# The attention stage of a hybrid decoder layer with its order written by hand, its scores negated, and other rules for the conditioning rows beside it

## The chip, the cores and the metric

The kernel runs on one NeuronCore of a Trainium2 chip. The metric is device time in microseconds (us). The kernel before takes 1560.94 us, the median of three runs (1560.8 to 1561.51). In what follows PE is the matrix engine (TensorE), PEld its weight loads, DVE the vector engine, ACT the scalar engine, SP the engine that issues nearly all loads from device memory.

## What is computed

One decoder layer on 256 tokens of width 2048, float32 throughout:

```
mod = silu(c) @ w_ada + b_ada            # 6 x 2048 numbers: shift, scale, gate, twice
h = adaLN(RMSNorm(x))
lru_x, lru_gate, q, k, v, g_a, g_b = split(h @ w_in)
rec = rg_lru(conv4(lru_x))               # two gate products a 128-channel block, then a scan over tokens
y_a = (rec * gelu(lru_gate)) @ w_lru_out
# attention: 32 query heads, 4 key heads of 64, blocks of 128 tokens, window 128
logits = q k^T * 64^-0.5 + bias          # or -1e30 outside the window
m = max(max(logits), sink);  e = exp(logits - m)
p = e / (sum(e) + exp(sink - m));  att = p v
y_b = att @ w_attn_out
x = x + gate1 * ((sigmoid(g_a) * y_a + sigmoid(g_b) * y_b) @ w_out)
x = x + gate2 * (relu(adaLN(RMSNorm(x)) @ w_ff1)^2 @ w_ff2);  out = RMSNorm(x)
```

## The kernel before

Every large product is split in three: weights and activations are each rounded to the fp32r type with a remainder, and high by high, high by low and low by high are summed in PSUM. A weight tile of 128 by 2048 numbers (1 MB) is loaded by SP into one of four `raw` buffers, rounded by ACT in two halves of 1024 columns (`wh`, line 177) and its remainder is taken by DVE in two halves (`wl`, line 182). There are four `wh` and four `wl` halves, enough for two tiles.

The work is a list of *units*, one weight tile each. Units 0 and 1 make k and v, units 2 to 9 eight pairs of q tiles, units 10 to 17 eight pairs of the recurrence's input (lx), units 18 to 25 its gate branch (lg), units 26 to 53 the two branch gates, 54 to 69 the product with w_lru_out (`ya`), then `yb`, `out`, and the MLP. Up to unit 29 a unit is 48 matmuls of 256 columns (`gemm`, lines 203 to 205): two halves of 24, one for each output tile, each reading one 1024-column half of the weights. From unit 30 on a unit is 16 matmuls of 512 columns and 16 of 256 (`gemm_wide`, lines 228 to 231). The split of `q` or `lx` between a first part, made in a stage ahead of the units, and the rest means that a unit ends with an addition to `both[f]`.

Beside the units stand two other kinds of work. **Side work** (`later`) is queued with a cost and taken from the queue after each unit as long as a credit of 2.3 a unit lasts, capped at 6: attention for one group of four heads at a time (`att_scores`, cost 2.5, and `att_values`, cost 0.3; eight groups), then for each of 16 recurrence tiles a convolution (line 738), two gate products (lines 746 and 747), a decay and a scan, and a gelu. **Rows** (`ada_dma`, `ada_unit`) make the 96 columns of `mod`: one load of 1 MB into a `raw` buffer and one DVE instruction of 2048 columns (line 282). A second credit sets how many rows are issued with a unit: 0.2 a unit up to unit 7, then 0.5, none in the two units ahead of `ya`, and what is left spread evenly after that. The first `ya` unit also splits the 16 results of the recurrence (line 166), and `flush()` ahead of it takes all side work that is left.

Each engine runs its instructions in the order of its own queue. The program is written in the order above, and a scheduler then sets each engine's order, except that instructions under `pin` keep the order in which they are written. In the units of the kernel before almost nothing is pinned.

Attention for one group of four heads (`att_scores`): 16 small matmuls on PE (line 666) give scores in four PSUM banks; eight DVE instructions (line 671) add the bias and take each row's running maximum; DVE negates the eight maxima (675) and subtracts them from the sink (676); ACT takes the exponential of that (677) and the eight exponentials with their sums (681); DVE adds, inverts (683, 684) and scales (688, eight instructions). In `att_values` PE transposes the four heads (703, twelve), ACT copies them to SBUF (705), PE multiplies with v (710, sixteen) and ACT copies the result (712).

## Time and profile before

| what | value |
|---|---|
| runs, median (lowest to highest) | 1560.94 us (1560.8 to 1561.51) |
| the profiled execution's own time | 1560.38 us |
| its span in the trace | 1558.6 us |
| PE busy | 1540.5 us, 99% of the span |
| DVE busy | 1287.1 us, 83% |
| ACT busy | 926.2 us, 59% |
| granted TensorE clock, mean | 0.998 |
| bytes moved | 387.93 MB, 249 GB/s on average |

Times in the trace are us from the span's start. A row of a group has the line of the kernel, the engine, the operation, what it writes and reads, its count, then busy time and the mean duration of one in ns, then the idle time of its engine ahead of it. A row of the list of waits says who waited for whom, how many us in total, how many times, and the longest. A row of the timeline has start, duration, engine, line and count, and in brackets how long the engine was idle ahead of it and what ended that. A row of windows has a stretch, its length, and for each engine the busy time and in brackets the number of instructions, then the granted clock, the share of the DMA engines and GB/s. Matmuls overlap: each lasts longer than the distance to the next one's start.

### The profile page before, as it was taken

What the parts mean: (1) busy time and instruction counts of PE and PEld (TensorE: products, weight loads), DVE (VectorE), ACT (ScalarE), POOL (GpSimd) and SP (SyncE); (2) the same over time, 40 slices, a digit from 0 to 9 for tenths busy, and PEclk for the clock granted to TensorE, in tenths of its full rate; (3) what the DMA queues carried; (4) which work ended last, traced back from release to release, by engine and by line L of the source; (5) the groups of instructions that cost most, each with busy time, mean ns of one, the idle gap of its engine ahead of it and who ended that gap; (6) DMA issues with size and microseconds to landing.
All of it is one profiled execution on the core that took longest, in us unless ns stands there. A gap on an engine that the chain in (4) does not pass through costs nothing.

```text
span 1558.6 us, 25695 instructions
## 1 busy us (share of the span) xinstructions
PE 1540.5 (99%) x10137; PEld 1396.9 (90%) x10137; DVE 1287.1 (83%) x2037; ACT 926.2 (59%) x1531; POOL 0.2 (0%) x4
## 2 busy tenths in 40 slices
PE   8999999999999999999999999999999999999998
PEld 7999999889988888888889988888988888888887
DVE  5898987889999888898898877888866887668885
ACT  5763456579886564444465763366744765357764
POOL 0000000000000000000000000000000000000000
PEclk9999999999999999999999999999999999999999
DMA  9999976545768777777876676865654556546551
GB/s 374 349 387 335 358 272 233 216 167 215 283 250 303 279 266 299 293 293 275 324 285 237 230 268 240 320 226 188 217 193 175 178 198 222 187 159 203 191 215 55
DMA packets 84744, 387.93 MB, mean 249 GB/s; under 512 B 7344, under 2 KB 36368, under 8 KB 44432
## 3 DMA queue, kind: packets, MB, share of 16 engines
q1 hardware_dynamic: 79632, 381.51, 67.3%
q10 hardware_dynamic: 4992, 4.79, 1.0%
q8 instruction: 79, 1.29, 0.3%
q14 instruction: 41, 0.34, 0.1%
HBM read 384.13 MB, written 2.15 MB: 248 GB/s over the span
## 4 chain that ended last, share of the span: by engine, by line
PE 92%; DVE 3%; DMA 2%; ACT 2%; issue 1%; SPq 0%; DVEq 0%; ACTq 0%
PE pg L229 41%; PE pg L228 20%; PE pg L205 5%; PE pg L203 5%; PE pg L204 5%; DMA ra<-in_wada_dram 1%; PE pg L231 1%; PE pa L938 1%; PE pa L940 1%; PE pa L939 1%; PE pg L985 1%; PE pg L986 1%; PE pg L987 1%; PE pa L710 1%; PE pa L703 1%
## 5 line engine op out<-in xcount | busy, mean ns | idle before, releaser
L229 PE MATMUL pg<-k,wh 128*128 128x512 f32 x2832 | 980.9, 394 | 1.1 <-DVE k L166 1.1
L177 ACT ACTIVATE wh<-rw 128x1024 fp32r<-128x1024 f32 (+1 forms) x542 | 560.2, 1041 | 481.1 <-PE pg L229 320.9
L182 DVE TENSOR_TENSOR wl<-rw,wh 128x1024 fp32r<-128x1024 f32 (+1 forms) x542 | 644.6, 1201 | 162.3 <-ACT wh L177 157.3
L228 PE MATMUL pg<-k,wl 128*128 128x256 f32 x2655 | 743.0, 280 | 0.0
L229 PEld LDWEIGHTS pg<-k,wh 128*128 128x128 f32 x2832 | 521.6, 188 | 107.4 <-issue 1.4
L228 PEld LDWEIGHTS pg<-k,wl 128*128 128x128 f32 x2655 | 499.0, 188 | 8.8 <-ACT k L165 0.7
L203 PE MATMUL pg<-k,wh 128*128 128x256 f32 x878 | 248.3, 283 | 0.0
L204 PE MATMUL pg<-k,wh 128*128 128x256 f32 x878 | 247.0, 282 | 0.0
L205 PE MATMUL pg<-k,wl 128*128 128x256 f32 x878 | 247.0, 282 | 0.0
L282 DVE CUSTOM_DVE_ANT_0 ra<-ra,scr,vc 128x2048 f32<-128x2048 f32 x96 | 225.3, 2347 | 12.0 <-DMA ra<-in_wada_dram 10.4
L203 PEld LDWEIGHTS pg<-k,wh 128*128 128x128 f32 x878 | 165.4, 188 | 1.9 <-issue 1.6
L205 PEld LDWEIGHTS pg<-k,wl 128*128 128x128 f32 x878 | 164.8, 188 | 1.7 <-issue 1.5
L204 PEld LDWEIGHTS pg<-k,wh 128*128 128x128 f32 x878 | 165.1, 188 | 0.6 <-issue 0.3
L1104 DVE SCALAR_TENSOR_TENSOR k<-pg,mod,k 128x256 f32<-128x256 f32 x100 | 48.3, 483 | 17.9 <-PE pg L229 16.4
L236 DVE TENSOR_TENSOR t<-pg,t 128x256 f32<-128x256 f32 x127 | 53.1, 418 | 0.5 <-ACT t L235 0.5
L231 PE MATMUL pg<-k,wl 128*128 128x256 f32 x177 | 49.6, 280 | 0.0
L235 ACT ACTIVATE t<-pg 128x256 f32<-128x256 f32 x127 | 46.3, 365 | 0.6 <-PE pg L229 0.6
L987 PE MATMUL pg<-z,wl 128*128 128x258 f32 x144 | 40.9, 284 | 0.0
L985 PE MATMUL pg<-z,wh 128*128 128x258 f32 x144 | 40.8, 284 | 0.0
L986 PE MATMUL pg<-z,wh 128*128 128x256 f32 x144 | 40.7, 283 | 0.0
L231 PEld LDWEIGHTS pg<-k,wl 128*128 128x128 f32 x177 | 33.4, 189 | 7.1
L166 DVE TENSOR_TENSOR k<-t,k 128x256 fp32r<-128x256 f32 x80 | 33.8, 422 | 1.9 <-ACT k L165 1.9
(216 smaller groups left out, 1351.6 us busy)
## 6 DMA issues: line engine op xcount, KB each, us to landing
rw<-in_w_f_dram SPq DMA_DIRECT2D x188, 1024.0 KB, 4.9
ra<-in_wada_dram SPq DMA_DIRECT2D x96, 1024.0 KB, 6.7
rw<-in_w_r_dram SPq DMA_DIRECT2D x30, 1024.0 KB, 5.0
rw<-in_w_p_dram SPq DMA_DIRECT2D x29, 960.0 KB, 6.9
rw<-in_w_f_dram SPq DMA_DIRECT2D x48, 256.0 KB, 3.3
bt<-ud ACTq DMA_DIRECT2D x8, 512.0 KB, 4.1
k<-in_w_p_dram SPq DMA_DIRECT2D x9, 256.0 KB, 10.8
lw<-in_lruw_dram SPq DMA_DIRECT2D x4, 512.0 KB, 5.7
```

The costliest lines, as they stand in the source:

```text
L177: pin(se.activation(wh[:, :c], raw[:, o:o + c], AF.Copy))
L182: pin(ve.tensor_tensor(out=wl[:, :c], in0=raw[:, o:o + c], in1=wh[:, :c].bitcast(F32), op=ALU.subtract))
L203: te.matmul(ps, lhsT=wh[:, w], rhs=hl[:, 0], start=k == 0, stop=False)
L204: te.matmul(ps, lhsT=wh[:, w], rhs=hl[:, 1], start=False, stop=False)
L205: te.matmul(ps, lhsT=wl[:, w], rhs=hl[:, 0], start=False, stop=k == n - 1)
L228: te.matmul(ps[:, 0], lhsT=wl[:, w], rhs=hl[:, 0], start=False, stop=False)
L229: te.matmul(ps, lhsT=wh[:, w], rhs=hl, start=k == 0, stop=k == n - 1)
L231: te.matmul(ps[:, 0], lhsT=wl[:, w], rhs=hl[:, 0], start=False, stop=False)
L282: pin(ve.tensor_tensor_reduce(out=raw, in0=raw, in1=scr, scale=1.0, scalar=vc[:, V_BADA + c:V_BADA + c + 1], op0=ALU.mult, op1=ALU.add, ac ...
L985: te.matmul(ps, lhsT=wh[:, e], rhs=z[k][:, 0:258], start=k == 0, stop=False)
L986: te.matmul(ps[:, 0:256], lhsT=wh[:, e], rhs=z[k][:, 258:514], start=False, stop=False)
L987: te.matmul(ps, lhsT=wl[:, e], rhs=z[k][:, 0:258], start=False, stop=k == KT - 1)
```

## The change

- **Attention in sixteen units.** Units 3 to 18 no longer go through the loop. `attention(ready)` writes eight groups, two units a group, with everything pinned: half of unit *a*, the scores, the second half of *a*, half of unit *b*, the transposes, the second half of *b*, the values. The rounding of the next group's weights, their remainders, their loads and one row stand at written places between. Before, eight groups were spread by credit over the units from 2 on and the scheduler set their place.
- **Scores negated.** q is scaled by -0.125, the bias line and the sinks are negated once, the DVE instruction takes a running minimum, and the result is the exponential's bias as it stands. The negation of eight maxima (line 675) is gone, and each exponential is written right behind its own DVE instruction; the exponential of the sink comes after the eight.
- **All transposes of a group together, all values together**, instead of two heads at a time.
- **Side work waits.** No side work is taken before unit 19; the credit stands at its cap of 6 by then. Attention is no longer in the queue.
- **Rows.** One a group in the attention units (eight), then 0.1 a unit up to unit 28 and 0.5 from unit 29 on; at most one a unit; none in the four units ahead of `ya` and its first three. By the loop's own arithmetic rows 1, 7, 16 and 28 fell in units 0 to 2, 3 to 18, 19 to 53 and 54 to 97; now it is 1, 8, 11 and 32, of which 13 fall one a unit in units 57 to 69.

The main parts of the diff:

```diff
-LAG, CC, CG, CV, CS = 2, 1.0, 0.6, 0.3, 2.5
+LAG, CC, CG = 2, 1.0, 0.6
+ATT, GROUPS, ATT_ROWS = 3, 8, [1] * 8
-LOOK, CREDIT, Z_FROM, ADA_RATE, ADA_SLOW, QUIET_ATT = 2, 2.3, 12, 0.5, 0.2, 8
+LOOK, CREDIT, Z_FROM, QUIET_YA = 2, 2.3, 12, 4
+ADA_RATES = 29 * [0.1] + 27 * [0.5]
...
-                    ve.tensor_tensor_reduce(out=s[:, sl], in0=pss[i][:, sl], in1=bt[:, 2 * t + i, 0:128 * (b + 1)],
-                                            scale=1.0, scalar=sink[:, c:c + 1], op0=ALU.add, op1=ALU.max,
-                                            accum_out=m[:, c:c + 1])
+                    pin(ve.tensor_tensor_reduce(out=s[:, sl], in0=pss[i][:, sl], in1=bt[:, 2 * t + i, 0:128 * (b + 1)],
+                                                scale=1.0, scalar=sink[:, c:c + 1], op0=ALU.add, op1=ALU.min,
+                                                accum_out=ng[:, c:c + 1]))
+                    table("exp", pin(se.activation(s[:, sl], s[:, sl], AF.Exp, scale=-1.0, bias=ng[:, c:c + 1],
+                                                   accum_out=dn[:, c:c + 1])))
...
+    def attention(ready):
+        nxt = {n: Half(n) for n in range(ATT + 2, ATT + 2 * GROUPS + 2)}
...
+        for g in range(GROUPS):
+            a, b = ATT + 2 * g, ATT + 2 * g + 1
+            for _ in range(ATT_ROWS[g]):
+                ada_dma(pin)
...
+            half(a, 0)
+            att_scores(g)
+            att_sink(g)
+            if g + 1 < GROUPS:
+                att_bias(g + 1)
+            half(a, 1)
+            fin(a)
+            att_scale(g)
+            na, nb = first(g + 1), second(g + 1)
+            na.round()
+            na.round()
+            half(b, 0)
+            att_turns(g)
+            na.rest()
+            na.rest()
+            if first(g + 2):
+                first(g + 2).ask()
+            for _ in range(ATT_ROWS[g]):
+                ada_unit(pin)
+            nb.round()
+            half(b, 1)
+            fin(b)
+            att_values(g)
+            nb.round()
+            nb.rest()
+            nb.rest()
+            if second(g + 2):
+                second(g + 2).ask()
...
+        if n == ATT:
+            stage[0] = pin
+            attention(ready)
+            stage[0] = same
+        if ATT <= n < ATT + 2 * GROUPS:
+            continue
...
-        if not (n_ya - 2 <= n < n_ya or n_ff1 - QUIET_OUT <= n < n_ff1 or n_ff1 + 16 - QUIET_FF1 <= n < n_ff1 + 16):
-            while ada_credit > rows and ada_next[0] + rows < 6 * KT:
+        if not (n_ya - QUIET_YA <= n < n_ya + 3 or n_ff1 - QUIET_OUT <= n < n_ff1 or n_ff1 + 16 - QUIET_FF1 <= n < n_ff1 + 16):
+            while ada_credit > rows and rows < 1 and ada_next[0] + rows < 6 * KT:
...
-        while credit > 0 and side:
+        while credit > 0 and side and n >= ATT:
```

**How the orders differ at three places.** First DVE, in the seventh group, from the last score instruction to the first scaling. `as` holds a group's maxima, sums and inverses, `wl` is a weight remainder, `ra` a row, `k_607<-pg_3821` a unit's closing addition. Before:

```order
L671 ISA t_3368,as_3346<-pa_3360,bt_3344,vc 128x256
L671 ISA as_3346 128x1
L182 TENSOR_TENSOR wl_3815<-rw_3811,wh_3813 128x1024
L675 TENSOR_SCALAR as_3346<-as_3346 128x8
L676 TENSOR_TENSOR as_3346<-vc,as_3346 128x8
L282 ISA ra_4044,mod<-ra_4044,scr,vc 128x2048
L282 ISA mod 128x1
L773 TENSOR_TENSOR k_607<-pg_3821,k_607 128x512
L683 TENSOR_TENSOR as_3346<-as_3346 128x8
L684 RECIPROCAL as_3346<-as_3346 128x8
L688 TENSOR_SCALAR t_3353<-t_3353,as_3346 128x128
```

and now:

```order
L683 ISA t_3774,as_3746<-pa_3764,bt_3575,nsink 128x256
L683 ISA as_3746 128x1
L693 TENSOR_TENSOR as_3746<-as_3746,nsink 128x8
L852 TENSOR_TENSOR k_668<-pg_3721,k_668 128x512
L699 TENSOR_TENSOR as_3746<-as_3746 128x8
L700 RECIPROCAL as_3746<-as_3746 128x8
L704 TENSOR_SCALAR t_3753<-t_3753,as_3746 128x128
```

The weight remainder and the row have left the stretch between scores and scaling; they stand behind the eight scalings now.

Second PE, at the transposes (`idt`) and values (`vtok`) of the sixth group; `wh`/`wl` rows are a unit's matmuls. Before:

```order
L205 MATMUL pg_3821<-k_1669,wl_3664 128x256
L703 MATMUL pa_3309<-idt,t_3207 128x128
L203 MATMUL pg_3821<-k_1766,wh_3662 128x256
L204 MATMUL pg_3821<-k_1766,wh_3662 128x256
L703 MATMUL pa_3309<-idt,t_3207 128x128 x2
L703 MATMUL pa_3315<-idt,t_3210 128x128 x3
```

and now (the second group, alike in all eight):

```order
L206 MATMUL pg_2792<-k_2207,wl_2683 128x256
L712 MATMUL pa_2817<-idt,t_2723 128x128 x3
L712 MATMUL pa_2823<-idt,t_2728 128x128 x3
L712 MATMUL pa_2829<-idt,t_2739 128x128 x3
L712 MATMUL pa_2835<-idt,t_2744 128x128 x3
L204 MATMUL pg_2792<-k_1175,wh_2681 128x256
```

Twelve transposes stand in one block at the middle of unit *b*, and 24 of that unit's matmuls lie between them and the values.

Third DVE ahead of the first `ya` unit, where the splits of the recurrence's results (`k_6450<-k_531` and after) begin. Before:

```order
L282 ISA ra_6436,mod<-ra_6436,scr,vc 128x2048
L282 ISA mod 128x1
L182 TENSOR_TENSOR wl_6345<-rw_6341,wh_6343 128x1024
L182 TENSOR_TENSOR wl_6349<-rw_6341,wh_6347 128x1024
L236 TENSOR_TENSOR t_6384<-pg_6351,t_6384 128x256
L282 ISA ra_6438,mod<-ra_6438,scr,vc 128x2048
L282 ISA mod 128x1
L182 TENSOR_TENSOR wl_6393<-rw_6389,wh_6391 128x1024
L166 TENSOR_TENSOR k_6450<-k_531,k_6450 128x256
```

and now:

```order
L183 TENSOR_TENSOR wl_6325<-rw_6317,wh_6323 128x1024
L237 TENSOR_TENSOR t_6360<-pg_6327,t_6360 128x256
L872 SCALAR_TENSOR_TENSOR t_6365<-t_6365,k_940 128x256
L183 TENSOR_TENSOR wl_6375<-rw_6371,wh_6373 128x1024
L874 SCALAR_TENSOR_TENSOR t_6365<-t_6365,k_940 128x256
L167 TENSOR_TENSOR k_6428<-k_532,k_6428 128x256
L875 SCALAR_TENSOR_TENSOR k_723<-t_6365,k_723 128x256
```

The two rows are gone from there, and the last steps of the last gelu (872, 874, 875) stand where none stood before.

More of the change, by code (lines that the diff above doesn't have):

```diff
@@ L404, in hybrid_layer @@
     relt = cp.tile([32, NH], F32, name="relt")
+    nsink = cp.tile([P, 2 * NH], F32, name="nsink")
     ud = dp.tile([32, 384], F32, name="ud")
@@ L646, in hybrid_layer, with att_bias @@
     ast = {}
+    stage = [same]
+    keep = lambda i: stage[0](i)
+    def att_bias(g):
+        bt = sp.tile([P, 4, T], F32, tag="bias", name=nm("bt"), bufs=1)
+        pin(se.dma_start(out=bt, in_=bass.AP(tensor=ud.tensor, offset=ud.offset + 4 * g * 384,
+                                             ap=[[1, P], [384, 4], [1, T]])))
+        ast[g] = bt
     def att_scores(g):
         kv = g // 2
-        bt = sp.tile([P, 4, T], F32, tag="bias", name=nm("bt"), bufs=1)
-        se.dma_start(out=bt, in_=bass.AP(tensor=ud.tensor, offset=ud.offset + 4 * g * 384,
-                                         ap=[[1, P], [384, 4], [1, T]]))
-        st = sp.tile([P, 4, 8], F32, tag="ast", name=nm("as"), bufs=2)
-        m, ng, dn, es = st[:, 0], st[:, 1], st[:, 2], st[:, 3]
+        bt = ast[g]
+        st = sp.tile([P, 3, 8], F32, tag="ast", name=nm("as"), bufs=2)
+        ng, dn = st[:, 0], st[:, 1]
         ss = []
-        sink = vc[:, V_SINK + 8 * g:V_SINK + 8 * g + 8]
+        sink = nsink[:, 8 * g:8 * g + 8]
         for t in range(2):
@@ L680, in att_scores @@
                 c = 2 * i + b
-                table("exp", se.activation(ss[i][:, sl], ss[i][:, sl], AF.Exp, bias=ng[:, c:c + 1],
-                                           accum_out=dn[:, c:c + 1]))
-        ve.tensor_tensor(out=dn, in0=dn, in1=es, op=ALU.add)
-        ve.reciprocal(out=dn, in_=dn)
-        for i in range(4):
-            for b, sl in HALVES:
-                c = 2 * i + b
-                ve.tensor_scalar(out=ss[i][:, sl], in0=ss[i][:, sl], scalar1=dn[:, c:c + 1], scalar2=None, op0=ALU.mult)
@@ L689, in att_scores, with att_turns @@
-        ast[g] = ss
+                pin(ve.tensor_scalar(out=ss[i][:, sl], in0=ss[i][:, sl], scalar1=dn[:, c:c + 1], scalar2=None,
+                                     op0=ALU.mult))
+    def att_turns(g):
+        pvs = []
+        for s in ast[g][0]:
+            pt = bank([P, 384])
+            for n, j in enumerate((0, 2, 1)):
+                pin(te.transpose(pt[:, n * P:(n + 1) * P], s[:, j * P:(j + 1) * P], idt))
+            pv = tmp([P, 384])
+            pin(se.activation(pv, pt, AF.Copy))
+            pvs.append(pv)
+        ast[g] = pvs
@@ L708, in att_values @@
             for kb, cols, pc in ((1, slice(0, 256), slice(0, 256)), (0, slice(128, 256), slice(256, 384))):
                 for i in range(2):
-                    te.matmul(po[64 * i:64 * i + 64, cols], lhsT=vtok[:, kb, vs], rhs=pvs[i][:, pc],
-                              start=kb == 1, stop=kb == 0)
-            se.activation(res[F_Q + 2 * g + t], po, AF.Copy)
-    def q_fin(f, ps, part):
-        ve.scalar_tensor_tensor(out=part, in0=ps, scalar=0.125, in1=part, op0=ALU.mult, op1=ALU.add)
-        if f > 0:
-            later(CV, att_values, f // 2 - 1)
-        later(CS, att_scores, f // 2)
-        if f == 14:
-            later(CV, att_values, 7)
+                    pin(te.matmul(po[64 * i:64 * i + 64, cols], lhsT=vtok[:, kb, vs], rhs=pvs[2 * t + i][:, pc],
+                                  start=kb == 1, stop=kb == 0))
@@ new lines, in attention, with half, fin @@
+    def attention(ready):
+        nxt = {n: Half(n) for n in range(ATT + 2, ATT + 2 * GROUPS + 2)}
+        first, second = lambda g: nxt.get(ATT + 2 * g), lambda g: nxt.get(ATT + 2 * g + 1)
+        first(1).ask()
+        second(1).ask()
+        att_bias(0)
+        for g in range(GROUPS):
+            a, b = ATT + 2 * g, ATT + 2 * g + 1
+            for _ in range(ATT_ROWS[g]):
+                ada_dma(pin)
+            ps = {}
+            def half(n, i):
+                f = pairs[n][0]
+                if i == 0:
+                    ps[n] = pg.tile([P, 2, T], F32, tag="pg", name=nm("pg"))
+                acts = h[_done(f):]
+                gemm(ready[n], i * len(acts), acts, ps[n][:, i], pin)
+            def fin(n):
+                f, fn = pairs[n][:2]
+                fn(f, ps[n], both[f])
+                ready[n] = None
+            half(a, 0)
[26 more added lines that the diff above has]
+                second(g + 2).ask()
+            ready[na.n], ready[nb.n] = na.parts, nb.parts
@@ L723, in hybrid_layer @@
+    def q_fin(f, ps, part):
+        keep(ve.scalar_tensor_tensor(out=part, in0=ps, scalar=-0.125, in1=part, op0=ALU.mult, op1=ALU.add))
     lw, ri, ys, cv = {}, {}, {}, {}
@@ L772, in lx_fin @@
             later(2.0, softplus)
-        ve.tensor_tensor(out=part, in0=ps, in1=part, op=ALU.add)
+        keep(ve.tensor_tensor(out=part, in0=ps, in1=part, op=ALU.add))
         if j % 4 == 2:
```

60 lines of the change are left out of this document (36 added, 24 removed).

## The prediction

> **What bounds the kernel now.** I read the page's busy times first, then the windows, then who waited, and last the timeline at the waits.
>
> ```profile
> PE 1540.5 (99%) x10137; PEld 1396.9 (90%) x10137; DVE 1287.1 (83%) x2037; ACT 926.2 (59%) x1531; POOL 0.2 (0%) x4
> ```
>
> PE is busy for all but 18 us. The change moves work between 217 and 568 us, so the stages there count; beside them one stretch of pure matmuls as a yardstick:
>
> ```profile
> 80.00:120.00 40.00, 40.00 (x342) 40.00 (x341) 38.36 (x42) 23.49 (x34) 0.00 (x0) 1.00 0.98 387
> ...
> 217.00:337.00 120.00, 118.61 (x991) 106.74 (x991) 95.65 (x278) 76.10 (x212) 0.00 (x0) 1.00 0.57 204
> 337.00:446.00 109.00, 106.64 (x803) 102.33 (x802) 107.78 (x197) 93.90 (x156) 0.00 (x0) 1.00 0.65 239
> 446.00:548.00 102.00, 102.00 (x587) 89.52 (x586) 92.69 (x138) 67.59 (x121) 0.00 (x0) 1.00 0.77 287
> 548.00:568.00 20.00, 18.94 (x109) 16.44 (x108) 15.49 (x20) 12.93 (x26) 0.00 (x0) 1.00 0.81 302
> ```
>
> PE idles 1.4 us in the attention stretch (217 to 337), 2.4 in the recurrence stretch (337 to 446, where DVE is busy 107.8 of 109), nothing to 548, and 1.1 at the first ya unit. A 256-column matmul starts every 40/342 = 0.117 us but lasts 0.28, so an idle gap hides more than it shows:
>
> ```profile
> 316.18 0.29 PE L204 MATMUL pg<-k,wh 128*128 128x256 f32 x1
> 316.30 0.28 PE L205 MATMUL pg<-k,wl 128*128 128x256 f32 x1
> 316.99 0.33 PE L703 MATMUL pa<-idt,t 128*128 128x128 f32 x1 [0.41 <-DVE t L688]
> ```
>
> Start to start it is 0.69 us where 0.117 would do: 0.57 lost, 0.41 of it shown as idle. I add 0.16 us to each wait. The waits by name, of the three stretches in turn:
>
> ```profile
> PEld pa L710 <- ACT t L705: 2.1, 10, 0.2
> PE pa L703 <- DVE t L688: 1.3, 3, 0.5
> ...
> PE pa L746 <- DVE t L738: 2.1, 2, 1.3
> PE pa L746 <- ACT t L766: 0.2, 1, 0.2
> ...
> PE pg L229 <- DVE k L166: 1.1, 1, 1.1
> ```
>
> So the whole of what better order can win here is a handful of waits: transposes waiting for scaled scores, values waiting for copied transposes, recurrence gates waiting for their convolution, and the first ya unit waiting for its splits. All else is matmul time, which the change leaves as it is.
>
> **The change part by part.**
>
> *Transposes.* 1.3 + 3 x 0.16 = **1.8 us** lost before. The cause is on DVE:
>
> ```profile
> 277.39 1.58 PE L666 MATMUL pa<-kd,k 64*128 64x128 f32 x16
> 278.35 0.35 DVE L671 CUSTOM_DVE_ANT_0 t<-pa,bt,vc 128x128 f32<-128x128 f32 x1 [0.68 <-PE pa L666]
> 280.65 0.48 DVE L671 CUSTOM_DVE_ANT_0 t<-pa,bt,vc 128x256 f32<-128x256 f32 x1
> ...
> 311.05 1.22 DVE L182 TENSOR_TENSOR wl<-rw,wh 128x1024 fp32r<-128x1024 f32 x1
> 312.34 2.35 DVE L282 CUSTOM_DVE_ANT_0 ra<-ra,scr,vc 128x2048 f32<-128x2048 f32 x1
> 312.57 0.39 ACT L681 ACTIVATE t<-t,as 128x128 f32<-128x128 f32 x1
> 315.59 0.49 ACT L681 ACTIVATE t<-t,as 128x256 f32<-128x256 f32 x1
> 316.21 0.17 DVE L683 TENSOR_TENSOR as<-as 128x8 f32<-128x8 f32 x1 [0.91 <-ACT t L681]
> 316.41 0.20 DVE L684 RECIPROCAL as<-as 128x8 f32<-128x8 f32 x1
> 316.65 1.93 DVE L688 TENSOR_SCALAR t<-t,as 128x128 f32<-128x128 f32 x8
> ```
>
> From the last score instruction (311.05) to the first scaling (316.65) pass 5.6 us: a weight remainder, then the exponentials one after the other. Now each exponential follows its own score instruction. With t = 0 at the scores' start: score instructions from 0.96 (278.35 - 277.39), eight in 2.7, done at 3.7; exponentials from 1.4, eight in 3.6 (312.57 to 316.17), then the sink's, about 0.2, done at 5.2; sum and inverse 0.44 (316.21 to 316.65), first scaling at 5.65; the four heads are scaled at 6.1, 6.6, 7.1 and 7.6 (1.93/4 each). PE meanwhile runs the scores (1.5, from 277.39 to the next matmul below at 278.90), half of a and half of b (24 x 0.117 = 2.8 each) and about 0.2 of changes between kinds, and reaches the transposes at 7.3; the last head is wanted 1.0 later (nine transposes at 0.11), at 8.3. Cover is left over, 0.7 us for the last head. I keep 0.3 us for misses in eight groups and gain 1.5.
>
> *Values.* Before, the second two heads' values came right behind their copies:
>
> ```profile
> 274.24 0.92 PE L710 MATMUL pa<-t,vtok 128*64 128x256 f32 x8
> 275.08 0.87 PE L703 MATMUL pa<-idt,t 128*128 128x128 f32 x6
> ...
> 276.36 1.11 PE L710 MATMUL pa<-t,vtok 128*64 128x256 f32 x8
> 277.39 1.58 PE L666 MATMUL pa<-kd,k 64*128 64x128 f32 x16
> 278.90 0.39 PE L203 MATMUL pg<-k,wh 128*128 128x256 f32 x1
> ```
>
> The first block takes 0.84 to the next start, the second 1.03. 0.19 x 8 groups = **1.5 us**; now half a unit (2.8 us) lies between copies and values, and all of it goes.
>
> *What is late next in these units?* DVE has per group 2.7 (scores) + 1.9 (scaling) + 0.5 (small ones) + two closing additions at about 0.65 + four remainders at 1.16 (below) + a row at 2.3 = 13.3 us, PE 4 x 2.8 + 1.5 + 1.3 (transposes, twice 275.71 - 275.08) + 1.7 = 15.7 us. The second remainder of b ends last: its rounding waits for ACT's copies of the values. By these durations it is done some 1 us before DVE is wanted for the next scores. The row's load is issued some 10 us before its instruction and needs, from issue to landing in the median, the 6.7 us of its row on the page:
>
> ```profile
> ra<-in_wada_dram SPq DMA_DIRECT2D x96, 1024.0 KB, 6.7
> ```
>
> The bias load is issued a whole group ahead, as before. The negated sinks cost one small instruction, and eight fall away: nothing.
>
> *Recurrence gates.* Lost before: 2.3 in 3 waits + 3 x 0.16 = **2.8 us**. One of them on the timeline, then three remainders in a row, then two starts a unit apart from the chain of waits:
>
> ```profile
> 394.20 2.45 DVE L738 SCALAR_TENSOR_TENSOR t<-k,vc,t 128x253 f32<-128x253 f32 x6
> 394.95 1.28 ACT L750 ACT_TABLE_LOAD   x1
> 396.24 0.47 ACT L750 ACTIVATE t<-pa,vc 128x256 f32<-128x256 f32 x1
> 396.31 0.70 PE L746 MATMUL pa<-t,lw 128*128 128x256 f32 x2 [1.27 <-DVE t L738]
> ...
> 273.58 3.49 DVE L182 TENSOR_TENSOR wl<-rw,wh 128x1024 fp32r<-128x1024 f32 x3
> ...
> 655.14 0.47 PE pg L229 x2
> 660.73 0.46 PE pg L229 x2
> ```
>
> DVE was full, so the convolution came late. After the change this work lies in units 19 to 53, 35 units of 5.58 us (660.73 - 655.14), with 32 gate matmuls about 203 us of PE. DVE has there 70 remainders x 1.16 (3.49/3) = 81 us, 11 rows at 2.3 = 25, convolutions 48 x 0.41 (2.45/6) = 20, the rest of the recurrence and gelu an estimated 45 and the additions 15: 186 us start to start, some 205 counted by whole durations. That is 92 to 101% of PE's time, where it was 99% over 109 us. So most of the waits should shrink but not all: bounds 0 and the full 2.8 (or more, the rival below), I take that a third stays, 0.9, gain 1.9.
>
> *The first ya unit.* Lost: 1.1 + 0.16 = **1.3 us**.
>
> ```profile
> 550.37 5.90 SPq L108 DMA_DIRECT2D ra<-in_wada_dram  x2
> 556.16 2.35 DVE L282 CUSTOM_DVE_ANT_0 ra<-ra,scr,vc 128x2048 f32<-128x2048 f32 x1
> 558.43 0.08 DVE L282 DVE_READ_ACCUMULATOR2_ANT mod<- 128x1 f32 x1
> ```
>
> Two rows issued at 550 stood ahead of the splits on DVE, 2.3 us each (556.16 to 558.43). They go; a gelu's last steps come in their place, under 1 us. The splits after the fourth still stand behind unit 53's closing addition, so I keep 0.4 and gain 0.9.
>
> *Rows later.* 32 instead of 28 rows fall in units 54 to 97, the first 13 one a unit. DVE then has 2 x 1.16 + 2.3 and three 256-column instructions, about 5.6 us against 5.58; two tiles of lead cover the difference. I take 0.3 us lost.
>
> Sum: 1.5 + 1.5 + 1.9 + 0.9 - 0.3 = 5.5 us. 1560.38 (the profiled execution) - 5.5 = 1554.9; the median of the runs is 0.56 higher, so **1555.4 us**.
>
> **The rivals.**
>
> *More is won (1552.5).* By the two orders the stretches of small matmuls in the unit stage fall from 50 to 35. If each change of kind costs up to the 0.19 seen at the values, 15 x 0.19 = 2.9 more. Against it: the values are the one place where such a price shows, and there it is a wait. Chance 0.08.
>
> *Gates wait more (1560 and up).* One mechanism: DVE at 101% in units 19 to 53, so the gate matmuls catch up with the convolutions. The new order has 11 stretches of gate matmuls; at the mean of the three waits, 2.8/3 = 0.93, six waiting stretches cost 5.6 instead of 0.9, which gives 1560.1; all eleven, 10.2, give 1564.7. It is slower than before from seven on. For it: the DVE sum; against it: from 446 to 548 DVE is busy 92.7 of 102 and PE loses nothing. ACT has seven more table loads in its order, at 1.28 each 9 us, beside PE. The Trainium skill (ScalarE: Activation LUTs, What ACT_TABLE_LOAD costs) puts a switch of sets at about 2.66 us, 1.28 of load and 1.38 of drain; by it the seven would be 18.6 us. Here the next activation starts 0.01 after the load (394.95 + 1.28), so the drain does not show. Chance 0.12 for no change, 0.07 for slower.
>
> *The chain outlasts its cover (slower).* Place: the transposes in all eight groups, with everything pinned, so a late one stops PE. If first scaling stays 5.6 us behind the last score instruction instead of 2.0, the excess over cover is 3.6 - 0.7 = 2.9, times 8 = 23 us: 1578. It decides from a chain 1.4 us longer than I worked out (0.7 + 5.5/8). Chance 0.06.
>
> *Rows one a unit are too much for the loads (1558 to 1561).* A row and a tile are 2.1 MB in 5.58 us, 376 GB/s; the busiest window above moved 387 at a share of 0.98. If the units stretch to 5.8 us, 13 x 0.2 = 2.6 us go: 1558.0. The Trainium skill (DMA: Bandwidth & Descriptors, Where 436 GB/s comes from) puts the limit of a core's device memory at about 358 GB/s. By it a unit would take 5.86 us and 13 units 3.6 us more, 1559.0; the window of 387 speaks against it. Chance 0.07.
>
> **How the numbers follow.** The forecast has 0.60, with its own range 1552 to 1558. Changes under 0.2% (3.1 us) can't be told from none, so faster means below 1557.8. Faster: nearly all of 0.60, 0.08 and a part of the loads' case, 0.69. Same: 0.12, most of the loads' case and an edge of the forecast, 0.19. Slower: the gates' 0.07 and the chain's 0.06, rounded to 0.12. The range 1550 to 1564 leaves the chain and the worst of the gates outside.
>
> **What would show it.** Transposes and values without waits for scaling or copying, first scaling about 2 us behind the last score instruction, and a pitch of groups near 15.9 us would show the first two terms right. Gate matmuls with fewer or shorter idle gaps, and DVE below 97% between unit 19 and ya, the third. No row's load in the chain at the first ya unit, the fourth. A wait at the transposes in every group, gate gaps as long as before, or PE idle in the 70 us after the first three ya units would make it wrong.

## The result and the profile after

The changed kernel takes **1552.26 us** (median of six runs, 1551.69 to 1555.0) where the kernel before took 1560.87 in the same session. The ratio is 0.9948, with a 95% interval of 0.9935 to 0.996: 8.6 us won where 5.5 were forecast. The profiled execution took 1553.18 us with a span of 1551.4. Its granted clock was 0.5 from 17.5 to 24.4 us, where the trace of before has 1.00 and the work is the same; its first 60 us lose 1.7 us more than before, so the spans (1558.6 and 1551.4) show less of the gain than the medians.

The windows of the changed kernel, cut at its own stages: the yardstick of pure matmuls, attention (217 to 347), the recurrence in two parts, the first `ya` unit, and the stretch of rows one a unit.

```profile
80.00:120.00 40.00, 40.00 (x342) 40.00 (x341) 38.15 (x42) 24.04 (x35) 0.00 (x0) 1.00 0.99 388
217.00:347.00 130.00, 130.00 (x1140) 121.16 (x1140) 107.97 (x283) 81.93 (x218) 0.00 (x0) 1.00 0.64 231
347.00:446.00 99.00, 98.07 (x715) 92.66 (x714) 87.47 (x159) 82.81 (x134) 0.00 (x0) 1.00 0.60 221
446.00:541.00 95.00, 94.18 (x538) 82.50 (x537) 88.59 (x143) 77.27 (x134) 0.00 (x0) 1.00 0.74 263
541.00:568.00 27.00, 26.35 (x151) 22.89 (x150) 22.54 (x48) 21.91 (x51) 0.00 (x0) 1.00 0.49 184
568.00:640.00 72.00, 72.00 (x414) 63.22 (x414) 69.12 (x88) 33.47 (x48) 0.00 (x0) 1.00 0.90 333
```

PE is busy for all 130 us of attention. It still idles 0.9 and 0.8 us in the recurrence and 0.65 at the first `ya` unit. The rows one a unit cost PE no idle time. DVE, which I had put at 92 to 101% of the recurrence stretch, is at 88% (87.47 of 99) and 93% (88.59 of 95).

One group on the timeline, the second of eight. PE's rows first (scores, transposes, values, the next matmul, the next group's scores), then DVE's (last score instruction, closing addition of *a*, scalings):

```profile
236.31 1.58 PE L678 MATMUL pa<-kd,k 64*128 64x128 f32 x16
243.59 1.48 PE L712 MATMUL pa<-idt,t 128*128 128x128 f32 x12
247.82 1.52 PE L725 MATMUL pa<-t,vtok 128*64 128x256 f32 x16
249.27 0.39 PE L204 MATMUL pg<-k,wh 128*128 128x256 f32 x1
252.29 0.93 PE L678 MATMUL pa<-kd,k 64*128 64x128 f32 x8
...
239.57 0.48 DVE L683 CUSTOM_DVE_ANT_0 t<-pa,bt,nsink 128x256 f32<-128x256 f32 x1
240.96 0.69 DVE L799 SCALAR_TENSOR_TENSOR k<-pg,k 128x512 f32<-128x512 f32 x1 [0.70 <-PE pg L206]
242.00 1.93 DVE L704 TENSOR_SCALAR t<-t,as 128x128 f32<-128x128 f32 x8
```

No bracket stands at the transposes or the values. From scores to scores pass 15.98 us, and so it is from each group to the next; this distance is called the pitch below. The first scaling starts 5.69 us after the scores and 2.0 us after the last score instruction ended (239.57 + 0.48).

To see what each kind of small matmul cost, I summed over the whole trace the time from each one's start to the next matmul's start ("inside"). I added by how much the interval of the unit's matmul just ahead of a block, and of the first one behind it, exceeded what its shape takes in the yardstick ("ahead" holds the waits). All in us, before and after:

```
             inside           ahead          behind         all       saved
scores     12.09 -> 12.09   0.09 -> 0.73   0.86 -> 0.84  13.04->13.66  -0.6
transposes  9.25 ->  9.84   2.75 -> 0.0    2.32 -> 0.68  14.32->10.5    3.8
values     16.25 -> 11.61   1.90 -> 0.74   0.11 -> 0.86  18.26->13.21   5.0
gates      11.50 -> 12.24   3.15 -> 2.46   2.75 -> 2.06  17.40->16.76   0.6
```

The wait at the first `ya` unit went from 1.23 to 0.82 us, 0.4 saved. From 570 to 740 us 0.15 us is lost. All matmuls between 210 and 570 us together exceed the yardstick by 12.5 us where it was 21.0, 8.5 less. So attention gave nearly everything, and inside it the values most.

### The profile page after: what moved, and what is told of

Same layout as the page of the kernel before. It is cut to its first block, busy times and chain, and to the rows that moved or that the text cites. A ratio compares the mean times of both kernels' runs of the same rounds, so it can differ in the third digit from the quotient of the medians.

```text
span 1551.4 us, 25653 instructions
## 1 busy us (share of the span) xinstructions
PE 1536.2 (99%) x10137; PEld 1394.9 (90%) x10137; DVE 1286.0 (83%) x2030; ACT 932.7 (60%) x1538; POOL 0.2 (0%) x4
## 4 chain that ended last, share of the span: by engine, by line
PE 95%; ACT 3%; DMA 1%; DVE 1%; issue 0%; SPq 0%; DVEq 0%; ACTq 0%
PE pg L230 41%; PE pg L229 20%; PE pg L204 6%; PE pg L205 6%; PE pg L206 6%; PE pg L232 1%; PE pa L1017 1%; PE pa L1019 1%; PE pa L1018 1%; PE pg L1066 1%; PE pg L1065 1%; PE pg L1064 1%; PE pg L370 1%; ACT wh L178 1%; DMA ra<-in_wada_dram 1%; PE pa L678 1%
## 5 line engine op out<-in xcount | busy, mean ns | idle before, releaser
L236 ACT ACTIVATE t<-pg 128x256 f32<-128x256 f32 x127 | 46.6, 367 | 24.4 <-PE pg L230 24.4
L686 ACT ACTIVATE t<-t,as 128x128 f32<-128x128 f32 x64 | 28.4, 445 | 22.3 <-DVE as L683 22.3
```

## The experiments

All times are medians of five rounds or more beside the kernel before (1560.7 to 1561.0), and are compared with the 1552.26 us of the change. The runs of one kernel spread over 1 to 4 us (8.5 in one), and the first 60 us of a trace, the same work in every kernel, differ by up to 1.7 us in what they lose. Where less than 2 us matters I go by the trace. The diffs are cut to their main lines, and the comments in them are added.

### What made the values slow: blocks or waits

```diff
-            half(b, 1)
+            piece(b, 1, 0, 5)        # 15 matmuls of b's second half
+            att_values(g, (0,))      # first two heads
+            piece(b, 1, 5, 8)        # the other 9
             fin(b)
-            att_values(g)
+            att_values(g, (1,))
```

> The changed kernel with the values of a group in two blocks again, as before: the first two heads after 15 matmuls of b's second half, the other two after the remaining 9. Nothing waits for a copied transpose: the copies of the first two heads end about 1.9 us before their values. Times against 1552.3 us of the changed kernel. Theory 'waits' (the values of before were slow because the two heads of a pair waited for their own copies, so that the pair's matmuls did not start together): only the eight added blocks' entries and exits cost, 0.209 - 0.117 = 0.09 us each way, 8 x 0.18 = 1.4 us, so 1553.7, and a pair's two matmuls still start 7 ns apart. Rival 'blocks' (two short blocks instead of one long one are what cost): the whole 4.6 us that the values gained goes back, 1557, and each block of eight takes 0.84 to 1.03 us to the next start instead of half of 1.45.

Measured: 1555.47 us (ratio 0.9964, 0.9951 to 0.9976). The pitch is 16.33 us, 0.35 more, and 8 x 0.35 = 2.8 us, between the two theories. The values' inside sum is 12.81 us, 0.80 for each of the 16 blocks; the other 0.20 a group lies at the ends of the added block.

```diff
-            att_turns(g)
+            att_turns(g, (0,))
+            piece(b, 1, 0, 2)        # 6 matmuls
+            att_values(g, (0,))
+            att_turns(g, (1,))
+            piece(b, 1, 2, 3)        # 3 matmuls
+            att_values(g, (1,))
...
-            half(b, 1)
+            piece(b, 1, 3, 8)
             fin(b)
-            att_values(g)
```

> The changed kernel with the order of before at this place alone: transposes of two heads, 6 matmuls, their values, transposes of the other two heads, 3 matmuls, their values, all behind b's first half. Now the values do wait for their copies, and the transposes are in two blocks as well. Theory 'waits': the 4.6 us of the values go back, the second block being the slower one, and 16 added changes into and out of a block at 0.09 + 0.09 us add 2.9: 1552.3 + 4.6 + 2.9 = 1559.8; the two matmuls of a pair start 50 ns or more apart. Rival 'blocks': 4.6 for the values' two blocks and 0.18 x 8 = 1.4 for the added block of transposes, 1558.3, whether or not pairs start together. The prediction's own size (1.5 for the values, nothing for blocks): 1553.8.

Measured: 1558.07 us (ratio 0.9983, 0.9975 to 0.9992). The values' inside sum is 15.99 us, nearly the 16.25 of the kernel before. PE's timeline of this kernel, one group:

```profile
246.12 0.91 PE L726 MATMUL pa<-t,vtok 128*64 128x256 f32 x8
246.96 0.87 PE L714 MATMUL pa<-idt,t 128*128 128x128 f32 x6
...
248.11 1.23 PE L726 MATMUL pa<-t,vtok 128*64 128x256 f32 x8
249.27 0.39 PE L772 MATMUL pg<-k,wh 128*128 128x256 f32 x1
```

and of the kernel with the values apart:

```profile
247.73 0.87 PE L725 MATMUL pa<-t,vtok 128*64 128x256 f32 x8
248.53 0.38 PE L204 MATMUL pg<-k,wh 128*128 128x256 f32 x1
```

Without a wait a block of eight takes 0.80 us to the next start, here 0.84 and 1.16. The starts of the single matmuls say why. The two heads of a block write 64 columns each. With copies long done they start 7 ns apart; in the two blocks above the second head starts 0.05 and 0.36 us behind the first. 0.80 + 0.05 and 0.80 + 0.36 are the two blocks. The second head comes late because its copy does. The kernel before, seventh group, PE's and then ACT's timeline:

```profile
320.79 1.25 PE L710 MATMUL pa<-t,vtok 128*64 128x256 f32 x8
321.98 0.71 PE L666 MATMUL pa<-kd,k 64*128 64x128 f32 x6
...
320.25 0.88 ACT L705 ACTIVATE t<-pa 128x384 f32<-128x384 f32 x2
```

The two copies run from 320.25 to 321.13. The first head starts at 320.79, the second at 321.18, 0.39 later, and the block takes 1.19 = 0.80 + 0.39.

So the values lost in two ways: 16 x 0.216 = 3.4 us for second heads that came late (mean block 1.016 less 0.80), and 12.81 - 11.61 = 1.2 us for two blocks instead of one. Both theories hold a part; waits the larger. In time the undone order lost 5.8 us, against 7.5 ("waits") and 6.0 ("blocks"): of the 0.74 us that its pitch of 16.72 is longer, 0.55 lie inside the values and 0.19 at the ends of blocks, where "waits" had 0.36.

### The chain from scores to scaling, and its cover

```diff
             att_scores(g)
+            first(g + 1).round()     # one of the two roundings that stood behind the scalings
             att_sink(g)
...
-            na.round()
             na.round()
```

> The changed kernel with one weight rounding (about 1.0 us on ScalarE) written ahead of the sink's exponential in each group, so that the scalings start 1.0 us later; everything else in the same order. Theory 'cover' (the prediction's 0.7 us of slack for the last head's transposes; the trace of the change gives 0.65): 1.0 - 0.65 = 0.35 us lost in each of eight groups, 2.8 us: 1555.1, pitch of the groups 16.33 instead of 15.98 us, with an idle gap at the transposes. Rival 'slack elsewhere' (the matmuls ahead of the transposes are not what covers the chain, or the scalings overlap the transposes): no change, 1552.3, pitch 15.98.

Measured: 1553.45 us (ratio 0.9957, 0.9943 to 0.997). On the timeline of the fifth group:

```profile
283.62 1.58 PE L678 MATMUL pa<-kd,k 64*128 64x128 f32 x16
290.89 1.67 PE L712 MATMUL pa<-idt,t 128*128 128x128 f32 x12
299.80 1.57 PE L678 MATMUL pa<-kd,k 64*128 64x128 f32 x15
...
290.14 1.93 DVE L704 TENSOR_SCALAR t<-t,as 128x128 f32<-128x128 f32 x8
```

The first scaling comes 6.52 us after the scores, 0.82 later than in the change, since the sum had been waiting some 0.2 us for *a*'s closing addition anyway. The transposes still start 7.27 us after the scores, but their block has grown by 0.19 us, and the pitch is 16.18. So the slack is 0.82 - 0.19 = **0.63 us**. Theory "cover" holds; the expected size was off by the 0.2 that the addition hid. No bracket shows the wait: it lies between the transposes of one block.

```diff
+        pin(ve.tensor_scalar(out=held, in0=ng, scalar1=1.0, scalar2=None, op0=ALU.mult))
...
-                    table("exp", pin(se.activation(s[:, sl], s[:, sl], AF.Exp, scale=-1.0, bias=ng[:, c:c + 1],
-                                                   accum_out=dn[:, c:c + 1])))
...
+                table("exp", pin(se.activation(ss[i][:, sl], ss[i][:, sl], AF.Exp, scale=-1.0, bias=held[:, c:c + 1],
+                                               accum_out=dn[:, c:c + 1])))
```

> The changed kernel with the written order kept, but the exponentials made to wait for all eight score instructions, as the sum of all maxima made them before: one small VectorE copy of the eight minima stands between (about 0.17 us). By the trace of the change the last score instruction ends 0.4 us after its start and the eight exponentials take 3.6 us behind it, so the first scaling comes 2.3 us later than now. Theory 'cover': 2.3 - 0.65 = 1.65 us lost in each of eight groups, 13 us: 1565.5, slower than the kernel before, pitch about 17.6 us. Rival 'order alone' (the written order pays without the shorter chain): 1552 to 1554.

Measured: 1568.34 us (ratio 1.0049, 1.0036 to 1.0062), slower than the kernel before. Fifth group:

```profile
294.35 1.58 PE L678 MATMUL pa<-kd,k 64*128 64x128 f32 x16
302.89 2.08 PE L717 MATMUL pa<-idt,t 128*128 128x128 f32 x12 [1.10 <-DVE t L709]
...
302.54 1.93 DVE L709 TENSOR_SCALAR t<-t,as 128x128 f32<-128x128 f32 x8
```

First scaling at 8.19 us, 2.50 later; less 0.63 that is 1.87, and the pitch is 17.86, 1.88 more. All groups but the first have it; the first pitch is 21.96. There DVE waits 4.25 us for the load of the bias line, and the first score instruction starts only at 222.58, 3.74 us behind the scores (about 1 us elsewhere). PE then stands before the transposes (4.14 us from start to start), and the granted clock is 0.5 from 230.99 to 234.41. This profiled execution took 1570.69 us, 2.35 more than the median; eight groups at 1.88 alone would make 1567.3. The written order without the shorter chain is a loss.

The other half alone, in the kernel before:

```diff
+    nsink = cp.tile([P, 2 * NH], F32, name="nsink")
...
-                                            scale=1.0, scalar=sink[:, c:c + 1], op0=ALU.add, op1=ALU.max,
-                                            accum_out=m[:, c:c + 1])
+                                            scale=1.0, scalar=sink[:, c:c + 1], op0=ALU.add, op1=ALU.min,
+                                            accum_out=ng[:, c:c + 1])
+                    table("exp", se.activation(s[:, sl], s[:, sl], AF.Exp, scale=-1.0, bias=ng[:, c:c + 1],
+                                               accum_out=dn[:, c:c + 1]))
```

> The kernel before with only the negated scores, the running minima and each exponential behind its own score instruction; order, rows and rates as before. Theory 'order' (the values gained because the written order puts half a unit between copies and values, and the shorter chain is only what lets that order run without a wait): at most the transposes' 1.8 to 2.2 us, 1560.9 - 2 = 1559, and the values keep intervals near 16 us in sum. Rival 'chain' (the shorter chain alone frees the attention stretch): about 7 us, 1554.

Measured: 1566.64 us (ratio 1.0038, 1.0025 to 1.0051). Slower, which neither theory had. Seventh group:

```profile
294.08 1.58 PE L668 MATMUL pa<-kd,k 64*128 64x128 f32 x16
300.03 0.33 PE L701 MATMUL pa<-idt,t 128*128 128x128 f32 x1 [0.97 <-DVE t L686]
...
299.69 1.93 DVE L686 TENSOR_SCALAR t<-t,as 128x128 f32<-128x128 f32 x8
```

The chain is as short as in the change, first scaling 5.61 us after the scores. But the scheduler, which sets the order here, now has the transposes start 5.9 to 6.2 us behind the scores in five of the eight groups, where in the kernel before it was 9.3 to 11.6 in all, and seven of eight groups wait there for 0.65 to 1.4 us, start to start. What stands ahead of the transposes went from 2.75 to 7.76 us in sum, 5.0 of the 6.0 lost. It took the shorter chain as room to come earlier, and gave the cover away.

So the two parts are worth +6.0 us (chain alone), +7.7 (order alone, with the rows and the side work as changed) and -8.6 (both), each against the kernel before in its own session. Neither has a share of the gain of its own.

### Ends of blocks

```diff
             half(a, 0)
+            if g:
+                att_values(g - 1)
             att_scores(g)
...
             fin(b)
-            att_values(g)
```

> The changed kernel with the values of a group written directly ahead of the next group's scores, behind the next unit's first half, instead of ahead of that half: one stretch of small matmuls less in seven of eight groups, nothing else moved on PE. By the split of the values into two blocks (0.35 us a group for one block more, 0.15 of it inside the blocks and 0.20 at their ends) theory 'ends of blocks' expects 0.20 us less a group, a pitch of 15.78 instead of 15.98 and 7 x 0.2 = 1.4 us: 1550.9. Rival 'no price for ends': 15.98 and 1552.3. Against both: the scores' second pair of heads waits for the banks that the values hold, which would show as an idle gap inside the scores; 0.3 us each would make 1554.

Measured: **1550.69 us** (1550.36 to 1552.37; ratio 0.9934, 0.9922 to 0.9947), the fastest version here. Two groups:

```profile
265.06 1.52 PE L725 MATMUL pa<-t,vtok 128*64 128x256 f32 x16
266.51 1.58 PE L678 MATMUL pa<-kd,k 64*128 64x128 f32 x16
...
282.31 1.58 PE L678 MATMUL pa<-kd,k 64*128 64x128 f32 x16
```

The pitch is 15.80 to 15.81 us, 0.17 less, 1.2 us in seven groups. An end of a block has a price, and no bank made the scores wait. The intervals of its ratio and of the change's overlap, so that it beats the change rests on the pitch, not on the times alone. The block added above cost 0.20 at its ends, about the same. The Trainium skill (TensorEngine Tiling (Array Packing), Key Properties) says that changing the tiling mode drains TensorE. Beside it: values (128x64 tiles) and scores (64x128) pay 0.09 us each ahead of a block and transposes (full array) nothing, which agrees; but behind a block transposes pay 0.085 too, without a change of mode. The recurrence gates, full array too, pay nothing ahead and 0.19 behind. What is paid behind a block is thus not only the change of mode; no run here says whether the change of type makes it.

### What the gates still wait for

The change's timeline at a gate that waits, PE, DVE and ACT:

```profile
427.82 0.67 PE L825 MATMUL pa<-t,lw 128*128 128x256 f32 x2 [0.70 <-ACT k L890]
...
424.20 1.22 DVE L183 TENSOR_TENSOR wl<-rw,wh 128x1024 fp32r<-128x1024 f32 x1
425.33 0.42 DVE L237 TENSOR_TENSOR t<-pg,t 128x256 f32<-128x256 f32 x1
425.67 2.84 DVE L817 SCALAR_TENSOR_TENSOR t<-k,vc,t 128x253 f32<-128x253 f32 x7
...
426.91 0.42 ACT L890 ACTIVATE k<-t 128x256 f32<-128x256 f32 x1
```

The bracket names ACT's tanh, which had been done since 427.33. The seven convolution steps start 0.40 us apart; the fifth ends at 427.72, 0.10 us ahead of the gate, and it is the same at the other long wait (467.38 and 467.49). In DVE's order two convolutions alternate, so the first is done with the fifth step. The longest wait of the kernel before looks the same: in the prediction's rows six steps start at 394.20, the fifth ends at 396.26, and the gate starts at 396.31. (The expectation below says 60 ns and takes in a third, shorter wait; that one ends 0.26 us behind the nearest step and is left open.)

```diff
-            ve.scalar_tensor_tensor(out=y[:, d:], in0=xj[:, :T - d], scalar=cw(3 - d), in1=y[:, d:],
+            pin(ve.scalar_tensor_tensor(out=y[:, d:], in0=xj[:, :T - d], scalar=cw(3 - d), in1=y[:, d:],
```

> The changed kernel with the convolution steps of the recurrence kept in the order in which they are written: three steps of one convolution, then three of the next. In the changed kernel the planner interleaves two convolutions (first, first, second, second, third, third), so that the first is done with the fifth step, and its gate waits until 60 ns after that. Theory 'convolution': the first one is now done two steps, 0.8 us, earlier; the waits of 0.39, 0.87 and 0.98 us shrink by up to 0.8 each, 1.5 to 2 us in sum: 1550.5. The planner also moves some gates later, by up to half a unit, which by this theory helps too. Rival 'table load and banks' (the gates wait for ScalarE, as four in a row did where the sigmoid stood behind a table load): waits as before, 1552.3 or more.

Measured: 1553.93 us (ratio 0.9954, 0.9941 to 0.9966). The wait at the old last site fell from 0.98 to 0.28 us, but others came, 1.08, 1.62 and 1.00, and what stands ahead of the gates went from 2.46 to 4.14 us. The longest of them:

```profile
392.19 0.70 PE L825 MATMUL pa<-t,lw 128*128 128x256 f32 x2 [1.46 <-DVE t L817]
...
387.45 0.48 DVE L817 SCALAR_TENSOR_TENSOR t<-k,vc,t 128x253 f32<-128x253 f32 x1
387.85 2.35 DVE L283 CUSTOM_DVE_ANT_0 ra<-ra,scr,vc 128x2048 f32<-128x2048 f32 x1
390.12 0.48 DVE L817 SCALAR_TENSOR_TENSOR t<-k,vc,t 128x254 f32<-128x254 f32 x1
390.51 1.22 DVE L183 TENSOR_TENSOR wl<-rw,wh 128x1024 fp32r<-128x1024 f32 x1
```

Here the bracket names the convolution itself; its third step, at 391.65, ends 0.06 us ahead of the gate. That the gates wait for their convolution is shown; that the pin would shorten the wait was wrong, because the scheduler filled the places between dependent steps with a row and a remainder instead.

```diff
-            for i in range(j - 2, j + 2 + LAG):
-                if i <= j + 1:
-                    later(CC, lru_conv, i)
-                if i - LAG >= j - 2:
-                    later(CG, lru_gates, i - LAG)    # each gate two behind its own convolution
+            for i in range(j - 2, j + 2):
+                later(CC, lru_conv, i)
+            later(2.3, lambda: None)                 # a unit's credit left empty
+            for i in range(j - 2, j + 2):
+                later(CG, lru_gates, i)
```

> The changed kernel with the side work of the recurrence in another order: the four convolutions of a batch first, then one unit's credit left empty, then its four gates (before: a gate two convolutions behind its own); the credit of a unit is 2.55 instead of 2.3 so that all is done before the first ya unit. Theory 'convolution' (each remaining wait at the gates, 0.39, 0.87 and 0.98 us, ends 60 ns after the fifth of seven convolution steps that start behind a remainder and a closing addition on VectorE; four batches, one wait each): the waits go, 2.2 us: 1550.1. Rival 'table load' (the waits are named after ScalarE's tanh of the branch gates behind its 1.28 us table load): the waits stay at the sites where such a load stands ahead of the gates, 1552.3. Rival 'VectorE full': the waits move to other sites and stay at 2 us in sum.

Measured: 1556.14 us (ratio 0.9971, 0.996 to 0.9982). Two waits of 1.87 and 1.66 us, in blocks of four gates, of another kind:

```profile
400.31 0.59 PE L825 MATMUL pa<-t,lw 128*128 128x256 f32 x2
400.75 0.59 PE L826 MATMUL pa<-t,lw 128*128 128x256 f32 x2
403.28 0.70 PE L825 MATMUL pa<-t,lw 128*128 128x256 f32 x2 [1.71 <-ACT t L829]
...
401.46 1.28 ACT L829 ACT_TABLE_LOAD   x1
402.75 0.47 ACT L829 ACTIVATE t<-pa,vc 128x256 f32<-128x256 f32 x1
```

Two gates fill the four banks. The third waits until the first sigmoid has read its bank at 403.22, and that stands behind a table load. So the rival "table load" is right too, for blocks of more than two gates. The wait at the first `ya` unit also rose, to 1.54 us.

With the values at the scores and two gates at a time:

```diff
+            for i in range(j - 2, j + 2):
+                later(CC, lru_conv, i)
+            for i in range(j - 2, j + 2):
+                if i == j - 2:
+                    later(1.2, lambda: None)
+                if i == j:
+                    later(1.2, lambda: None)
+                later(CG, lru_gates, i)
```

> The kernel with the values directly ahead of the next scores (1550.69 us), and the recurrence's side work written as four convolutions, half a unit's credit empty, two gates, half a unit's credit empty, two gates; credit 2.45 instead of 2.3. What four gates in a row showed (the third gate waited 1.7 us for banks, which the sigmoids behind a table load had not yet freed) can't happen with two, since two gates take the four banks. Theory 'convolution' (a gate waits 60 ns past its own convolution's last step, and only because the steps stand shortly ahead of it): the waits at the gates, 2.2 us, go and 1548.5 us is left, if the denser credit costs nothing at the first ya unit. Rival 'ScalarE' (table loads ahead of sigmoids hold the banks in any order): the waits stay near 2 us in sum, 1550.7.

Measured: 1556.97 us (twelve runs, 1555.1 to 1563.58; ratio 0.9974, 0.9964 to 0.9983), 6.3 us slower than what it started from. Against 2.2 us in the kernel it started from, 1.6 are left ahead of the gates, nearly all in one wait of 1.59, where the scheduler set a third gate behind two again. But the work that came later now stands at the first `ya` unit:

```profile
556.70 0.47 PE L230 MATMUL pg<-k,wh 128*128 128x512 f32 x1 [1.32 <-DVE k L167]
559.41 0.79 PE L230 MATMUL pg<-k,wh 128*128 128x512 f32 x1 [1.55 <-DVE k L167]
```

From 545 to 570 us the trace loses 5.4 us more than that of the kernel it started from. Only part of it is in the two waits: from 558.76 to 565.59 the granted clock is 0.5, and matmuls of 512 columns start 0.43 us apart instead of 0.23. Moving the gates away from their convolutions, by a queue of credits, costs more at the end of the queue than it wins. The convolutions in turn together with the values at the scores:

> The convolutions in turn, and the values of a group directly ahead of the next group's scores. If the two are independent, what the second measured alone (1550.69 against 1552.26) and what the first is expected to bring add up: 1552.3 - 1.6 - 1.75 = 1549.0, pitch of the groups 15.81 us. By the rival on the gates 1550.7.

Measured: 1552.99 us (ratio 0.9948, 0.9935 to 0.996), pitch 15.81. The two were independent, as expected, but the one had nothing to give: 4.34 us ahead of the gates.

### The rows around the first `ya` unit

```diff
-        if not (n_ya - QUIET_YA <= n < n_ya + 3 or ...):
-            while ada_credit > rows and rows < 1 and ada_next[0] + rows < 6 * KT:
+        if not (n_ya - 2 <= n < n_ya or ...):
+            while ada_credit > rows and ada_next[0] + rows < 6 * KT:
```

> The changed kernel with the row rules of before put back: rows are held back only in the last two units ahead of the first ya unit, and a unit may take several. Rates and attention as changed. By the prediction's terms the first ya unit loses 0.9 us again and the units behind it win 0.3: 1552.9, with a row's instruction on VectorE ahead of the splits. Rival 'splits' (what is left at the first ya unit, 0.82 us, comes from the gelu steps and the closing addition ahead of the splits and not from rows): 1552.3 and the same 0.8 us gap.

Measured: 1556.86 us (ratio 0.9974, 0.9961 to 0.9986). The gap at the first `ya` unit is 3.95 us instead of 0.82:

```profile
563.50 0.77 PE L230 MATMUL pg<-k,wh 128*128 128x512 f32 x1 [3.78 <-DVE k L167]
...
557.40 2.34 DVE L283 CUSTOM_DVE_ANT_0 ra<-ra,scr,vc 128x2048 f32<-128x2048 f32 x1
```

That is 3.1 us more, and the time is 4.6 us more. Behind the gap, from 563.15 to 566.56, the granted clock is 0.5, which costs these 3.4 us some 1.7 more; neither the sum of the prediction nor the expectation had that.

> The changed kernel with one of the two row rules put back: rows are held back only in the last two units ahead of the first ya unit, but a unit still takes at most one. With both put back the time was 1556.86 and the gap at the first ya unit 3.95 us instead of 0.82, with rows at 551.5 and 557.4 us on VectorE ahead of the splits. Theory 'quiet' (the rows that were asked for within four units of the first ya unit are what stands ahead of the splits): a gap near 4 us, 1556. Rival 'one a unit' (several rows in one unit are the cause): a gap near 0.8 us, 1552.5.

With only the first of the two lines put back: 1554.29 us (1553.03 to 1556.25; ratio 0.9956, 0.9943 to 0.997). The gap is 0.59 us, no longer than in the change. The span is 1551.5, but the change's own span of 1551.4 has the slow clock of its first 60 us in it; behind 570 us this trace loses some 1.6 us more than the change's, a little everywhere and at no wait of its own, which stays open. So at the first `ya` unit "one a unit" is the rule that counts and the longer quiet is not. Why the change still waits there is on its own timeline, DVE and PE:

```profile
556.79 1.22 DVE L183 TENSOR_TENSOR wl<-rw,wh 128x1024 fp32r<-128x1024 f32 x1 [1.17 <-ACT wh L178]
557.93 0.42 DVE L874 SCALAR_TENSOR_TENSOR t<-t,k 128x256 f32<-128x256 f32 x1
558.27 0.42 DVE L167 TENSOR_TENSOR k<-k,k 128x256 fp32r<-128x256 f32 x1
...
558.83 0.47 PE L230 MATMUL pg<-k,wh 128*128 128x512 f32 x1 [0.65 <-DVE k L167]
```

No row: a remainder and a gelu's step stand ahead of the first split, and by the bracket DVE itself had stood idle for 1.17 us until ACT's rounding for that remainder was done.

## Why the prediction was right or wrong

The sign and the range held (1552.26 in 1550 to 1564, forecast 1555.4), and the cause named, a handful of waits in the order, is the one that the runs show for all but some 1.6 us of the gain. The sizes were off in both directions, and the time came nearer than its terms did: 5.8 us too little at transposes and values, 1.8 too much at gates and first `ya` unit, and 0.6 at the scores that it had not seen.

- **Transposes: right, too small.** Forecast 1.5 us, 3.8 measured. The chain came as worked out: first scaling 5.69 us after the scores (5.65), 2.0 us behind the last score instruction (2.0), transposes at 7.27 (7.3), slack 0.63 (0.7). The waits all went, 2.75 us rather than 1.8: the list of waits, from which the 1.8 came, leaves small ones out. The other 1.05 is the ends of blocks, which the sum had at nothing: 27 blocks became 8, so that 2.32 us behind them fell to 0.68, while the one long block takes 0.59 more inside.
- **Values: the term that was mis-sized, 5.0 us instead of 1.5.** The step that failed is "the first block takes 0.84 to the next start, the second 1.03; 0.19 x 8". It took one group, the second quickest, for all eight, and a block that itself waited as the yardstick. The 16 blocks of before took 0.85 to 1.18, 1.016 in the mean; without a wait a block takes 0.80, and in one run of sixteen matmuls 0.73.
- **Scores: left out.** Before, seven of eight stood directly behind values; now each has an entry of its own, 0.6 us lost.
- **Recurrence gates: a third of the forecast, 0.6 instead of 1.9.** The reason given, "DVE was full, so the convolution came late", does not hold in its first half for what is left: DVE is at 88 and 93% now and the longest waits are still 0.87 and 0.98 us. How much the full DVE added before is open. The convolution is late because its steps stand right ahead of the gate in DVE's order, behind a remainder and a closing addition, and alternate with the next convolution's.
- **First `ya` unit: 0.4 instead of 0.9.** The rows went as said; in their place stand the gelu's last step, which I named, and a remainder that waits for ACT, which I did not.
- **Rows later: 0.15 lost from 570 to 740, 0.3 forecast.**
- **The rivals.** "More is won (1552.5)" gave the measured time, at a chance of 0.08. Its mechanism, a price for each change of kind, is real: 0.17 to 0.20 us for both ends of a block, by two experiments, where the rival had 0.19. But it explains only 1.05 us at the transposes and 1.2 at the values, less the scores' 0.6, some 1.6 of the 2.9 that it needed. Waits do the rest: 3.4 us of second heads that came late, 2.75 at the transposes, 0.7 ahead of the gates, 0.4 at the first `ya` unit. That its time was met is in part luck. "Gates wait more" fell with DVE's 88%. "The chain outlasts its cover" did not happen, but the slack is as thin as said and its price is as worked out: 1.88 us a group for a chain 2.50 longer. "Rows too much for the loads" fell: 333 GB/s at a share of 0.90 from 568 to 640, and 371 at 0.97 in its busiest ten us (615 to 625), with PE busy for all 72 us.

## What to carry to other kernels

Shortening a chain and writing an order are worth something together: the shorter chain alone let the scheduler pull its consumer forward until it waited again, and the order alone made every group wait for the old chain. Price a block of small matmuls from a place where nothing waits, over all its instances and with its two ends; a pair that shares the array is as slow as its later half. Before moving work out of one wait, look at what its queue meets last.

## What the runs showed of the hardware that was not expected

- Two matmuls of 64 columns each, started 7 ns apart, run side by side: a block of two heads takes 0.80 us, and every 0.1 us by which the second head is late makes it 0.1 us longer (0.05 to 0.84, 0.36 to 1.16, 0.39 to 1.19). The later head's time is added whole. The list of waits had 0.2 us at most for one such wait, and only for the weight load. The Trainium skill (TensorEngine Tiling (Array Packing), Key Properties) says that tiles of the array work independently, weight loads and matmuls in parallel; the 7 ns starts agree with it.
- A matmul starts 0.06 to 0.10 us after what it waited for has ended (0.06 at 392.19 and 403.28 above, 0.10 at 427.82 and 467.49). Where the bracket named an engine that had been done for 0.5 us, this distance pointed to the convolution, which the bracket at 392.19 then named outright. The third wait, at 0.26, does not fit it.
- Behind a long stop of PE the granted clock was 0.5 for one or two spells of 3.41 us: behind 3.78 us idle from 563.15 to 566.56, behind the 4.14 us in the first group of the old chain from 230.99 to 234.41, and behind two waits of 1.32 and 1.55 us (at 556.70 and 559.41) from 558.76 to 565.59. A single wait of 1.71 us (at 403.28) had none. A spell costs about 1.7 us on top of the wait. That the stop brings the lower clock about is not tested here.
